# A hybrid decoder layer on one core: S5's four input tiles side by side, ahead of S5's tables

## The chip, the core and the metric

The kernel runs on one core of a Trainium2 chip. A core has a matrix engine (TensorE, here PE, with its weight loader PEld), a vector engine (VectorE, DVE), a scalar engine (ScalarE, ACT), a general engine (GpSimd, POOL) and a queue engine that issues most transfers (SyncE, SP). Each engine works through its own list of instructions; semaphores hold an instruction until what it reads is there. The metric is the time of one execution on the device in microseconds. The kernel before takes 1615.97 us, the median of three runs (1611.21 to 1623.19).

## The reference

One layer of a decoder trunk over a sequence of 1024 tokens of width 1024, all in float32. A normalised input is projected once; the columns of that projection feed an RWKV-7 branch, an S5 branch and two gates. The branches are merged, projected, normalised and added to the residual; a gated MLP with a short convolution follows. For the change only the first part matters:

```python
h = rms_norm(x, norm_mix_pre)
p = h @ w_in              # columns: RWKV's inputs | u (512 columns for S5) | two gates

def s5_branch(u, a_re, a_im, b_re, b_im, c_re, c_im, d, log_step, w_glu, b_glu):
    lam = lax.complex(a_re, a_im)
    dt = jnp.exp(log_step)[:, None]
    a_bar = jnp.exp(lam * dt)
    b_bar = ((a_bar - 1.0) / lam)[..., None] * lax.complex(b_re, b_im)
    ...
    _, states = lax.associative_scan(s5_combine, (a_elems, bu), axis=1)
    y = jnp.real(jnp.einsum('gcp,blgp->blgc', c, states)) + d * ug
```

`u` is 512 wide, that is four tiles of 128 channels. S5's coefficients (`a_bar`, its powers, `b_bar`, `c` times powers) depend on the parameters alone, not on x; the kernel calls what it derives from them "tables".

## The kernel before, in words

Activations lie transposed: 128 channels on the partitions, tokens along the row, in two halves of 512 tokens, `th` 0 and 1. A product of float32 accuracy is made from three matmuls of rounded operands: each operand is split into a high part (cast on ACT) and the low rest (a subtraction on DVE or POOL), and high x high, low x high and high x low are added in one PSUM bank (`mm3_steps`, the matmuls of L172, L173 and L174). So h of one half is eight tiles `hh` and eight `hl`, one pair for each of the eight k tiles of 128 channels, and a 128-column weight tile is `wh` and `wl`, each in two pieces of 512 (four k tiles apiece). The staging tile `wf` into which a piece is loaded has two buffers, `wh` and `wl` four each. An output tile of one half takes 8 x 3 = 24 matmuls of 128x512 into one of four banks called `gm`.

PE's order is written by a planner in the kernel; the other engines' order comes from a scheduler with priorities (HPN above HPW above HP2 above HP). The planner (`drive`, `background`, `drain`) runs **lanes** (generators that yield what a step costs on PE and how long to wait, the constants T_...) and puts **fill** between their steps: the list `self.fill` of generators, each step of it one k tile, three matmuls. `drain` runs fill until a condition holds.

The front half (`front_half`, from L1694) goes: norm of half 0, set-up and loading of S5's parameters, then a lane with the norm of half 1, during which fill begins. A norm squares x (ACT, sums of two on DVE), adds the squares over channels by matmuls with a column of ones (`sumsq`, L245), takes the root of the mean on DVE (`rstd`: L265, L136 to L141), spreads it over the partitions by matmuls (`spread`, L271), copies it out (`rbc`, L929) and scales x (L932), each tile then being split into `hh` (L226) and `hl` (L227). Fill begins with S5's input: `s5_in((0, 1))`, then `s5_in((2, 3))`, each of them two tiles of the first half of tokens, one behind the other, then the same two of the second; each tile's bank is copied out by ACT (`ev`, L1031), stored to `US`, and once both halves are stored, loaded again as `u8`. Behind it come `mix_in` (RWKV's input tiles), the gates' tiles, and the loads of the branch merge (`merge_loads`).

Behind the norm's lane stands `s5_setup`, many small DVE operations on 128x32 tiles, then S5's phase with two lanes: `tab_lane` makes tables (DVE from L508, transposes on PE at L544, L553, L598; trigonometry on DVE and ACT) and `s5_lane` runs the scan and the output products (L600 to L608 on DVE, L613 to L615 on PE). RWKV's phase follows (first matmul at L672, four "preps" and a chain; loads of its inputs go through ten buffers `ld`; last transposes of the output at L885), then the merge, the output projection, the next norm (L245 again), and the MLP.

Of the kernel before, what the change touches and what calls it, by code (L numbers as in the profile page):

```python
# [10 lines left out]
F32R = mybir.dt.float32r  # L11
# [7 lines left out]
D = 1024  # L19
T = 1024  # L20
NK = D // 128
# [50 lines left out]
class Kern:  # L72
# [68 lines left out]
            V.scalar_tensor_tensor(y, h, 1.5, y, ALU.add, ALU.mult)  # L141
        return y

    def load_w(self, *srcs):

        nc = self.nc
        wh, wl = [], []
        with self.tc.high_priority(HPW):
            for src in srcs:
                for o in range(0, src.shape[1], 512):  # L150
                    n = min(512, src.shape[1] - o)
                    h = self.wp.tile([128, 512], F32R, tag="wh", name=self.nm("wh"), bufs=NWH)
                    l = self.wp.tile([128, 512], F32R, tag="wl", name=self.nm("wl"), bufs=NWL)
                    f = self.wp.tile([128, 512], F32, tag="wf", name=self.nm("wf"), bufs=NWF)
                    nc.sync.dma_start(f[:, :n], src[:, o:o + n])
                    nc.scalar.copy(h[:, :n], f[:, :n])  # L156
                    nc.vector.tensor_tensor(l[:, :n], f[:, :n], h[:, :n].bitcast(F32), ALU.subtract)  # L157
                    wh.append(h)
                    wl.append(l)
        return wh, wl  # L160
# [753 lines left out]
    def norm(self, th, xs, pool):  # L914

        nc = self.nc
        ss = self.chk()[:, 0:512]
        yield 0, T_X
        for k in range(0, NK, 2):
            sq = [pool.tile([128, 512], F32, tag="sq", name=self.nm("sq"), bufs=4) for _ in range(2)]  # L920
            for i in range(2):
                nc.scalar.activation(sq[i], xs[k + i], AF.Square)
            nc.vector.tensor_tensor(sq[0], sq[0], sq[1], ALU.add)
            self.sumsq(ss, sq[0], k == 0)
            yield 0.9, 1.0
        bc = self.chk()[:, 0:512]
        self.spread(bc, self.rstd(ss, 1e-6, 1.0 / D))
        rbc = pool.tile([128, 512], F32, tag="rbc", name=self.nm("rbc"), bufs=1)
        nc.scalar.copy(rbc, bc)  # L929
        h = []  # L930
        for k in range(NK):
            nc.vector.scalar_tensor_tensor(xs[k], xs[k], self.vec("g_mix_pre", k), rbc, ALU.mult, ALU.mult)  # L932
            h.append(self.hsplit(xs[k], k, self.hp[th], eng=nc.gpsimd if k % 2 else nc.vector))
        self.h[th] = h
        yield 1.7, 5.0
# [84 lines left out]
        self.nc.sync.dma_start(self.u8[b], self.US[b].rearrange("i c g n -> (i c) g n"))  # L1020
        self.s5_in_done = b

    def s5_in(self, bs):

        w = [self.load_w(self.a["w_in"][14 + b]) for b in bs]
        for th in range(2):
            for b in bs:
                ps = self.gmp()
                yield from self.mm3_steps(ps, w[b % 2], 0, [h[0] for h in self.h[th]], [h[1] for h in self.h[th]])
                y = self.ev((128, 8, 64))  # L1030
                self.nc.scalar.copy(y.rearrange("p i n -> p n i"), ps.rearrange("p (n j) -> p n j", j=8)[:, :, ::-1])  # L1031
                self.nc.sync.dma_start(self.US[b].rearrange("i c g n -> (c g) i n")[:, :, th * 64:th * 64 + 64], y)
                if self.stored is not None:
                    self.load_u8(self.stored)
                    self.stored = None
                if th:
                    self.stored = b
# [656 lines left out]
    def front_half(self):  # L1694
# [7 lines left out]
        with tc.tile_pool(name="lxp", bufs=4) as self.lxp, tc.tile_pool(name="s5c", bufs=1) as self.s5c, \  # L1702
# [4 lines left out]
            with tc.tile_pool(name="xp", bufs=1) as xp:  # L1707
                with tc.high_priority(HPN):
                    xs = [self.load_x(0, xp)]
                    self.setup()  # L1710
                    self.s5w = {}
                    self.s5_load(0)
                    self.s5_load(1)
                    for _ in self.norm(0, xs[0], xp):
                        pass
                    xs.append(self.load_x(1, xp))
                self.fill = [self.s5_in((0, 1)), self.s5_in((2, 3)), self.mix_in()] + [self.gate_tiles(m) for m in range(14)] + [
                    self.merge_loads(), self.gate_tiles(14, 15)]
                self.outs, self.yr = 0, []
                self.drive([(HPN, self.norm(1, xs[1], xp))])  # L1720
                with tc.high_priority(HP):
                    self.s5_setup()
            with tc.tile_pool(name="s5p", bufs=1) as self.s5p:
# [63 lines left out]
                self.fill += [self.merge(mg), self.outproj(0, mg, self.mx0)]  # L1787


T_US, T_TAB0, T_TAB, T_TRIG, T_SCAN = 5.0, 38.0, 20.0, 12.0, 13.0  # L1790
T_LD, T_LT = 9.0, 3.0
NEVA = 4
T_KN, T_BK, T_GR, T_INV, T_LV, T_CH, T_LN = 5.0, 9.0, 2.5, 36.0, 1.0, 0.8, 11.0
T_X = 3.0
T_N0, T_RS, T_N1, T_N2, T_N4, T_N5, T_N3 = 2.5, 4.0, 2.2, 5.0, 1.6, 40.0, 2.0
NET = 5
MGAP = 1
# [2 lines left out]
NWH = 4  # L1800
NWL = 4
# [79 lines left out]
```

## Time and profile before

| what | value |
|---|---|
| median of three runs | 1615.97 us (1611.21 to 1623.19) |
| the profiled execution | 1613.51 us, of which its span 1611.7 us |
| mean granted clock of TensorE | 0.962 |
| PE busy | 1508.9 us (94%) |
| DVE busy | 1126.7 us (70%) |
| ACT busy | 696.8 us (43%) |
| POOL busy | 155.0 us (10%) |
| first matmul of S5's input | 25.92 us |
| S5's first table transposes (L544) | 106.2 us |
| RWKV's first product (L672) | 284.5 us |
| last transposes of RWKV's output (L885) | 781.4 us |

The profile is of one execution. A row of a timeline gives the start, the duration, the engine, the line, the operation, output and inputs, and in brackets the idle time before it with what ended it. A row of the stages gives from and to, the length, then for each engine the busy time with its count of instructions, then the clock granted to PE (1.00 is full speed), the busy share of the transfer engines and GB/s. A row of the waits gives what waited, for whom, and in total, how often and at longest. A matmul's duration overlaps the next one's, so the distance from start to start counts, not the duration.

### The profile page before, as it was taken

Reading aid. Unit: us, or ns where it says so; the run is one execution under the profiler, and the core shown is the slowest. Engines: PE = TensorE matmul, PEld = TensorE weight load, DVE = VectorE, ACT = ScalarE, POOL = GpSimd, SP = SyncE. Lnnn points to the kernel's source line nnn. Section 1 sums busy time; section 2 is a strip of 40 time slices with the busy share of each in tenths; the row PEclk is TensorE's granted clock in tenths of the full one; section 3 lists DMA queues with packets and bytes.
Section 4 is the critical chain, followed back from the end, with each engine's and each line's share of the span. In section 5 each row is a group of like instructions: output and inputs, shape, how many; then the busy total and the mean of one; then the engine's idle time right before and its main releaser. Section 6 shows DMA issues by size and latency. Waiting matters only on the chain. (4 is left out here: it accounts for less than half of the span.)

```text
span 1611.7 us, 26125 instructions
## 1 busy us (share of the span) xinstructions
PE 1508.9 (94%) x10028; PEld 1207.6 (75%) x10028; DVE 1126.7 (70%) x2039; ACT 696.8 (43%) x1109; POOL 155.0 (10%) x226
## 2 busy tenths in 40 slices
PE   5899899898999999889998999999999999999995
PEld 4688787686776776667866888788888887788784
DVE  5798774565365555865668579977777776788677
ACT  4345552224233344554443445554444444443451
POOL 2100001314123142010000000000000000000000
PEclk9799999999999999989988999999999999999997
DMA  5244334243352353552574453322222224963622
GB/s 178 63 140 142 98 113 169 65 136 117 106 153 94 97 171 107 171 156 93 190 223 156 144 190 125 124 79 83 90 89 78 78 87 142 321 215 106 229 84 104
DMA packets 133420, 213.84 MB, mean 133 GB/s; under 512 B 38656, under 2 KB 44800, under 8 KB 133296
## 3 DMA queue, kind: packets, MB, share of 16 engines
q1 hardware_dynamic: 124208, 188.32, 35.5%
q0 software_dynamic: 7936, 21.77, 4.6%
q10 hardware_dynamic: 1152, 2.10, 0.3%
q8 instruction: 78, 1.28, 0.3%
q14 instruction: 46, 0.38, 0.1%
HBM read 156.56 MB, written 53.48 MB: 130 GB/s over the span
## 5 line engine op out<-in xcount | busy, mean ns | idle before, releaser
L172 PE MATMUL gm<-hh,wh 128*128 128x512 f32 x688 | 299.6, 436 | 6.5 <-ACT hh L226 3.3
L173 PE MATMUL gm<-hl,wh 128*128 128x512 f32 x688 | 279.1, 406 | 5.4 <-DVE hl L227 4.5
L174 PE MATMUL gm<-hh,wl 128*128 128x512 f32 x688 | 276.6, 402 | 0.0
L156 ACT CAST wh<-wf 128x512 fp32r<-128x512 f32 x179 | 110.7, 620 | 196.7 <-PE gm L173 108.5
L157 DVE TENSOR_TENSOR wl<-wf,wh 128x512 fp32r<-128x512 f32 x179 | 124.8, 698 | 100.7 <-ACT wh L156 97.5
L172 PEld LDWEIGHTS gm<-hh,wh 128*128 128x128 f32 x688 | 134.0, 195 | 45.2 <-ACT hh L226 5.6
L173 PEld LDWEIGHTS gm<-hl,wh 128*128 128x128 f32 x688 | 134.2, 195 | 32.4 <-DVE hl L227 7.3
L174 PEld LDWEIGHTS gm<-hh,wl 128*128 128x128 f32 x688 | 134.1, 195 | 30.0
L1504 PE MATMUL d<-xl,wh 128*128 128x512 f32 x308 | 121.1, 393 | 3.3 <-DVE xl L227 3.3
L1503 PE MATMUL d<-xh,wh 128*128 128x512 f32 x308 | 120.8, 392 | 2.1 <-ACT xh L226 2.1
L1505 PE MATMUL d<-xh,wl 128*128 128x512 f32 x308 | 120.5, 391 | 0.0
L1329 PE MATMUL rp<-t,h 128*128 128x512 f32 x216 | 84.4, 391 | 1.9 <-ACT p L1343 1.9
L1331 PE MATMUL rp<-t,l 128*128 128x512 f32 x216 | 84.2, 390 | 0.5 <-DVE l L227 0.5
L1330 PE MATMUL rp<-t,h 128*128 128x512 f32 x216 | 84.1, 389 | 0.0
L1504 PEld LDWEIGHTS d<-xl,wh 128*128 128x128 f32 x308 | 58.1, 189 | 16.8 <-DVE xl L227 4.9
L1503 PEld LDWEIGHTS d<-xh,wh 128*128 128x128 f32 x308 | 58.2, 189 | 14.7 <-ACT xh L226 2.5
L1505 PEld LDWEIGHTS d<-xh,wl 128*128 128x128 f32 x308 | 58.2, 189 | 12.2
L226 ACT CAST h<-r 128x1024 fp32r<-128x1024 f32 x34 | 35.8, 1054 | 61.4 <-PE rp L1330 29.6
L227 DVE TENSOR_TENSOR l<-r,h 128x1024 fp32r<-128x1024 f32 x34 | 41.6, 1225 | 29.5 <-ACT h L226 28.0
L1350 DVE SCALAR_TENSOR_TENSOR y<-zv,vecs,y 128x1023 f32<-128x1023 f32 (+1 forms) x36 | 46.1, 1280 | 8.6 <-ACT y L1348 8.6
L1329 PEld LDWEIGHTS rp<-t,h 128*128 128x128 f32 x216 | 40.5, 188 | 11.4 <-ACT p L1343 2.7
L1331 PEld LDWEIGHTS rp<-t,l 128*128 128x128 f32 x216 | 40.5, 188 | 9.3 <-DVE l L227 1.0
(437 smaller groups left out, 3364.1 us busy)
## 6 DMA issues: line engine op xcount, KB each, us to landing
r<-in_w_up_dram SPq DMA_DIRECT2D x36, 512.0 KB, 3.2
wf<-in_w_in_dram SPq DMA_DIRECT2D x68, 256.0 KB, 2.9
st<-in_w_down_dram SPq DMA_DIRECT2D x55, 256.0 KB, 4.3
st<-ACT SPq DMA_DIRECT2D x44, 256.0 KB, 4.4
wf<-in_w_up_dram SPq DMA_DIRECT2D x36, 256.0 KB, 2.8
ACT<-y POOLq DMA_DIRECT2D x18, 512.0 KB, 2.9
GT<-ev SPq DMA_DIRECT2D x32, 256.0 KB, 2.3
wf<-in_w_br_dram SPq DMA_DIRECT2D x32, 256.0 KB, 3.1
```

The lines of the kernel that those rows point to most:

```text
L156: nc.scalar.copy(h[:, :n], f[:, :n])
L157: nc.vector.tensor_tensor(l[:, :n], f[:, :n], h[:, :n].bitcast(F32), ALU.subtract)
L172: mm(ps, a, xh[k], start=k == 0, stop=False)
L173: mm(ps, a, xl[k], start=False, stop=False)
L174: mm(ps, b, xh[k], start=False, stop=k == n - 1)
L1329: mm(ps, wh[:, c], xh, start=first and k == 0, stop=False, skip_group_check=True)
L1330: mm(ps, wh[:, c], xl, start=False, stop=False, skip_group_check=True)
L1331: mm(ps, wl[:, c], xh, start=False, stop=k == 3, skip_group_check=True)
L1350: V.scalar_tensor_tensor(y[:, lag:], z[:, 0:1024 - lag], self.vec(nme, i), y[:, lag:], ALU.mult, ALU.add)
L1503: mm(ps, wh[:, c], xh[:, x], start=start, stop=False, skip_group_check=True)
L1504: mm(ps, wh[:, c], xl[:, x], start=False, stop=False, skip_group_check=True)
L1505: mm(ps, wl[:, c], xh[:, x], start=False, stop=stop, skip_group_check=True)
```

## The change

`s5_in` handles all four tiles in one generator. It loads four weight tiles at the start (two of them into buffers of other pools: the high parts into the pool of x, the low parts into `lx` tiles), takes four banks for a half of the tokens, and goes over k outermost: at each k tile it steps through the four banks. When a half is done, the four banks are copied out and stored one behind the other. The norm's lane yields once between the root and its spread, with T_RS (4.0). After the norm's lane, fill is drained until the last tile of S5's input is finished, and only then comes `s5_setup`. Two constants change: the first wait of `norm`, T_X, and the first wait of the tables, T_TAB0.

```diff
-    def load_w(self, *srcs):
+    def load_w(self, *srcs, pool=None):
+        wp = pool or self.wp
...
-                    h = self.wp.tile([128, 512], F32R, tag="wh", name=self.nm("wh"), bufs=NWH)
-                    l = self.wp.tile([128, 512], F32R, tag="wl", name=self.nm("wl"), bufs=NWL)
+                    h = wp.tile([128, 512], F32R, tag="wh", name=self.nm("wh"), bufs=4 if pool else NWH)
+                    l = self.lx() if pool else wp.tile([128, 512], F32R, tag="wl", name=self.nm("wl"), bufs=NWL)
...
         bc = self.chk()[:, 0:512]
-        self.spread(bc, self.rstd(ss, 1e-6, 1.0 / D))
+        y = self.rstd(ss, 1e-6, 1.0 / D)
+        yield 0, T_RS
+        self.spread(bc, y)
...
-    def s5_in(self, bs):
-
-        w = [self.load_w(self.a["w_in"][14 + b]) for b in bs]
+    def s5_in(self, pool):
+
+        w = [self.load_w(self.a["w_in"][14 + b], pool=pool if b > 1 else None) for b in range(4)]
         for th in range(2):
-            for b in bs:
-                ps = self.gmp()
-                yield from self.mm3_steps(ps, w[b % 2], 0, [h[0] for h in self.h[th]], [h[1] for h in self.h[th]])
+            h = self.h[th]
+            ps = [self.gmp() for b in range(4)]
+            steps = [self.mm3_steps(ps[b], w[b], 0, [x[0] for x in h], [x[1] for x in h]) for b in range(4)]
+            for k in range(NK):
+                for b in range(4):
+                    yield next(steps[b])
+            for b in range(4):
+                next(steps[b], None)
                 y = self.ev((128, 8, 64))
-                self.nc.scalar.copy(y.rearrange("p i n -> p n i"), ps.rearrange("p (n j) -> p n j", j=8)[:, :, ::-1])
+                self.nc.scalar.copy(y.rearrange("p i n -> p n i"), ps[b].rearrange("p (n j) -> p n j", j=8)[:, :, ::-1])
...
-                self.fill = [self.s5_in((0, 1)), self.s5_in((2, 3)), self.mix_in()] + [self.gate_tiles(m) for m in range(14)] + [
+                self.fill = [self.s5_in(xp), self.mix_in()] + [self.gate_tiles(m) for m in range(14)] + [
                     self.merge_loads(), self.gate_tiles(14, 15)]
                 self.outs, self.yr = 0, []
                 self.drive([(HPN, self.norm(1, xs[1], xp))])
+                self.drain(lambda: self.stored == 3)
                 with tc.high_priority(HP):
                     self.s5_setup()
...
-T_US, T_TAB0, T_TAB, T_TRIG, T_SCAN = 5.0, 38.0, 20.0, 12.0, 13.0
+T_US, T_TAB0, T_TAB, T_TRIG, T_SCAN = 5.0, 20.0, 20.0, 12.0, 13.0
...
-T_X = 3.0
+T_X = 8.0
```

In the rows below a name's number tells one tile from another; in the kernel after the change the line numbers are higher by one up to L929, by three to about L1023 and by eight behind.

PE, the first matmuls of S5's input, before. `hh_301` and `hl_302` are the first k tile of h, `hh_306` and `hl_307` the second, `gm_381` the bank of the first output tile.

```order
L172 MATMUL gm_381<-hh_301,wh_357 128x512
L173 MATMUL gm_381<-hl_302,wh_357 128x512
L174 MATMUL gm_381<-hh_301,wl_358 128x512
L172 MATMUL gm_381<-hh_306,wh_357 128x512
L173 MATMUL gm_381<-hl_307,wh_357 128x512
L174 MATMUL gm_381<-hh_306,wl_358 128x512
```

PE at the same place, of the change (`gm_405` to `gm_408` are the four banks).

```order
L173 MATMUL gm_405<-hh_301,wh_357 128x512
L174 MATMUL gm_405<-hl_302,wh_357 128x512
L175 MATMUL gm_405<-hh_301,wl_358 128x512
L173 MATMUL gm_406<-hh_301,wh_369 128x512
L174 MATMUL gm_406<-hl_302,wh_369 128x512
L175 MATMUL gm_406<-hh_301,wl_370 128x512
L173 MATMUL gm_407<-hh_301,wh_381 128x512
L174 MATMUL gm_407<-hl_302,wh_381 128x512
L175 MATMUL gm_407<-hh_301,lx_382 128x512
L173 MATMUL gm_408<-hh_301,wh_393 128x512
L174 MATMUL gm_408<-hl_302,wh_393 128x512
L175 MATMUL gm_408<-hh_301,lx_394 128x512
```

A k tile of h is now read by twelve matmuls into four banks before the next one is wanted; before it was read by three.

ACT, from the copy of the spread root (`rbc`) of the second norm on, before: `hh_484` and those after it are the high parts of h's second half, `ev_424` and `ev_532` the copies of the first two banks.

```order
L1031 COPY ev_424<-gm_381 128x64x8
L929 COPY rbc_481<-chk_461 128x512
L388 ACT_TABLE_LOAD
L388 ACTIVATE sm_668<-sm_666 128x32
L389 ACTIVATE sm_670<-sm_666 128x32
L395 ACTIVATE sm_674<-sm_675 128x32
L390 ACTIVATE sm_669<-sm_670,hpi 128x32
L226 COPY hh_484<-x_340 128x512
L1031 COPY ev_532<-gm_427 128x64x8
L226 COPY hh_489<-x_342 128x512
L226 COPY hh_494<-x_344 128x512
```

ACT at the same place, of the change: `ev_603`, `606`, `609` and `612` are the copies of the four banks of the first half.

```order
L390 ACTIVATE sm_934<-sm_930 128x32
L391 ACTIVATE sm_933<-sm_934,hpi 128x32
L932 COPY rbc_543<-chk_505 128x512
L227 COPY hh_546<-x_340 128x512
L1039 COPY ev_603<-gm_405 128x64x8
L227 COPY hh_551<-x_342 128x512
L227 COPY hh_556<-x_344 128x512
L1039 COPY ev_606<-gm_406 128x64x8
L227 COPY hh_561<-x_346 128x512
L1039 COPY ev_609<-gm_407 128x64x8
L1039 COPY ev_612<-gm_408 128x64x8
L227 COPY hh_566<-x_348 128x512
```

The set-up's activations now stand ahead of `rbc`, and the four copies stand among the casts of h's second half.

DVE, where S5's tables begin, before: `sml` are the first products of the tables, `wl_914` a low part of a weight of RWKV's input.

```order
L508 TENSOR_TENSOR sml_824<-s_b_225,s5q_754 128x128
L509 TENSOR_TENSOR sml_825<-s_b_227,s5q_757 128x128
L557 TENSOR_TENSOR dg_1120<-csts,s5d 16x128
L510 TENSOR_TENSOR sml_821<-sml_824,sml_825 128x128
L157 TENSOR_TENSOR wl_914<-wf_915,wh_913 128x512
L508 TENSOR_TENSOR sml_829<-s_b_225,s5w_760 128x128
L509 TENSOR_TENSOR sml_830<-s_b_227,s5w_763 128x128
```

DVE at the same place, of the change (`wl_732` to `wl_1121` are the low parts of the first two weight tiles of RWKV's input).

```order
L475 TENSOR_SCALAR s5q_1005<-s5ai 64x288
L158 TENSOR_TENSOR wl_732<-wf_733,wh_731 128x512
L158 TENSOR_TENSOR wl_738<-wf_739,wh_737 128x512
L158 TENSOR_TENSOR wl_1115<-wf_1116,wh_1114 128x512
L158 TENSOR_TENSOR wl_1121<-wf_1122,wh_1120 128x512
L509 TENSOR_TENSOR sml_1020<-s_b_225,s5q_950 128x128
L510 TENSOR_TENSOR sml_1021<-s_b_227,s5q_953 128x128
L558 TENSOR_TENSOR dg_1217<-csts,s5d 16x128
```

Four weight pieces now stand in a row ahead of the tables' first product; before they stood among the products.

## The prediction

> **What bounds the kernel now.** I read the page's busy list first, then the stages, then the waits of the one stage that the change reorders.
>
> ```profile
> span 1611.7 us, 26125 instructions
> PE 1508.9 (94%) x10028; PEld 1207.6 (75%) x10028; DVE 1126.7 (70%) x2039; ACT 696.8 (43%) x1109; POOL 155.0 (10%) x226
> ```
>
> PE is the bound: 103 us of its span are idle or between instructions. The change adds and removes no matmul, so it can only win idle time or time at a lower clock. The stages (bounds chosen at the first matmul of h, the second norm's square sums, its scaling, the first unhindered matmul, S5's first table, RWKV's first product, its last transposes, the next norm):
>
> ```profile
> core 0: us, PE busy (x) PEld busy (x) DVE busy (x) ACT busy (x) POOL busy (x), PEclk, DMA share, GB/s
> 26.00:38.40 12.40, 10.69 (x29) 6.37 (x30) 12.40 (x15) 8.46 (x15) 5.62 (x4) 0.88 0.11 34
> 38.40:53.20 14.80, 14.35 (x52) 12.01 (x51) 8.29 (x74) 1.07 (x1) 0.48 (x1) 0.53 0.07 19
> 53.20:69.40 16.20, 11.30 (x34) 7.69 (x33) 14.58 (x35) 8.46 (x16) 5.56 (x4) 0.79 0.11 33
> 69.40:106.20 36.80, 36.80 (x164) 30.39 (x162) 35.34 (x90) 14.01 (x20) 0.89 (x2) 1.00 0.55 164
> 106.20:284.50 178.30, 168.07 (x926) 144.11 (x924) 124.08 (x188) 81.01 (x111) 13.54 (x22) 0.97 0.40 126
> 781.40:823.00 41.60, 38.25 (x157) 28.96 (x156) 22.84 (x33) 22.34 (x39) 0.00 (x0) 0.93 0.80 251
> ```
>
> The 43.4 us from 26.0 to 69.4 are the poor ones: PE busy 10.69, 14.35 and 11.30 us, clocks of 0.88, 0.53 and 0.79. Only 69 of S5's 192 input matmuls are done by 69.4. From there PE never stops and the clock is 1.00: 54 triplets' first matmuls in 36.80 us (next row), that is 162 matmuls at **0.2272 us**. That is the price of one "fill" matmul, the work the planner puts between the steps of a lane.
>
> ```profile
> 69.40:106.20 36.80, 21.04 (x54) 9.95 (x53) 1.00 0.55 164
> PE gm L173 <- DVE hl L227: 4.5, 5, 2.7
> PE gm L172 <- ACT hh L226: 3.3, 2, 2.1
> PE gm L173 <- POOL hl L227: 0.9, 1, 0.9
> PE chk L271 <- DVE sm L328: 0.5, 1, 0.5
> 45.65 0.63 PE L174 MATMUL gm<-hh,wl 128*128 128x512 f32 x1
> 46.08 0.63 PE L172 MATMUL gm<-hh,wh 128*128 128x512 f32 x1
> ```
>
> The waits (26 to 106 us) name h's halves as the releaser: 9.2 us with POOL's and the root's. The last two rows are 0.43 us apart: at the low clock a fill costs **0.427 us**.
>
> **The change, part by part.** *Where the fills go.* By the order, 231 fills stand ahead of S5's first transposes (L544) before and 285 after; ahead of the last output product of S5 (L613) 684 and 738; ahead of RWKV's first product (L672) 738 and 810; ahead of the last transposes L885 2049 and 2121; ahead of the next norm's square sums (L245) 2196 in both. So S5 and RWKV meet the same fills between their own steps, save 18 more just ahead of L672, and the last stretch has 72 fewer. The gain is therefore 72 x 0.2272 = 16.4 us, less what L885 comes later. I follow the delay to there.
>
> *First tile half (th0).*
>
> ```profile
> 25.92 0.79 PE L172 MATMUL gm<-hh,wh 128*128 128x512 f32 x1 [2.11 <-ACT hh L226]
> 27.20 0.80 PE L173 MATMUL gm<-hl,wh 128*128 128x512 f32 x1 [0.48 <-DVE hl L227]
> 34.22 0.95 PE L245 MATMUL chk<-ones,sq 128*128 128x1 f32 x8
> 38.82 1.70 PE L245 MATMUL chk<-ones,sq 128*128 128x1 f32 x8
> 49.09 0.16 DVE L265 TENSOR_SCALAR rv<-chk 128x4 f32<-128x4 f32 x1 [6.24 <-PE chk L245]
> 52.28 1.19 PE L271 MATMUL chk<-csts,rsy 128*128 128x128 f32 x8 [0.45 <-DVE sm L328]
> 54.12 2.08 DVE L932 SCALAR_TENSOR_TENSOR x<-x,vecs,rbc 128x512 f32<-128x512 f32 x3
> L157 DVE TENSOR_TENSOR wl<-wf,wh 128x512 fp32r<-128x512 f32 x179 | 124.8, 698 | 100.7 <-ACT wh L156 97.5
> ```
>
> Four more weight tiles are split ahead of h's scaling; two of their four lows stand among DVE's x rows, 0.7 us each, so I let the second matmul start at 27.9 instead of 27.2 (bounds 27.2 and 30.0, all four in series). Then each k brings 12 matmuls (2.7 us warm) where before it brought 3, and h's lows before came 1.6 us apart or less on average (the second at 27.2, the eighth's wait over at 37.80): after the first k nothing waits for h. Eleven fills at 0.427 lead to 32.6, the rest of the 96 at 0.2272 to 51.7; four square-sum groups at 0.95 and the spread at 1.19 make 56.7, with small change **57.1**. The root: its new wait of T_RS puts 24 fills (5.5 us) between the last square sums and the spread; on DVE it took from 49.09 to about 52.1 before, 3.0 us. So the root is covered, 0.5 us of wait goes, and what queues behind the spread on PE (6 fills, then the next tile's) waits for nothing new.
>
> *Bank handover.* DVE works through S5's small set-up ahead of the scaling of x (row 166 there, row 126 before). Spread at about 53, plus the copy of rbc, plus those rows, puts that scaling at 55.0, against 54.12: no earlier h for th1. And the four banks of th1 are those of th0, so each waits for its copy out:
>
> ```profile
> 56.06 0.60 ACT L226 CAST hh<-x 128x512 fp32r<-128x512 f32 x1
> L1031 ACT COPY ev<-gm x8: 1061/1092/1107, 42.0 to 99.2; 128x512 f32<-128x512 f32 x8
> ```
>
> ACT's order there is hh, copy, hh, hh, copy, hh, copy, copy. With 0.60 a cast (the first done at 56.3) and 1.09 a copy, they end at 57.4, 59.7, 61.4 and 62.5; the first k of th1 ends at **63.2** instead of 59.8, a new loss of 3.4 us. Behind it 84 x 0.2272 gives the 192nd fill at **82.3**; before it was 69.4 + 123 x 0.2272 = 97.3. L544 stands 93 fills on: **103.4**, against 106.2 (54 fills fewer).
>
> *S5's tables.* On DVE four weight lows now stand ahead of the tables.
>
> ```profile
> L156 ACT CAST wh<-wf 128x512 fp32r<-128x512 f32 x179 | 110.7, 620 | 196.7 <-PE gm L173 108.5
> wf<-in_w_in_dram SPq DMA_DIRECT2D x68, 256.0 KB, 2.9
> 76.83 0.29 DVE L508 TENSOR_TENSOR sml<-s_b,s5q 128x128 f32<-128x128 f32 x1
> 90.83 1.35 DVE L533 TENSOR_TENSOR ca<-ca,ct 128x1152 f32<-128x1152 f32 x1
> 131.61 1.23 DVE L600 TENSOR_TENSOR t<-chk,t 128x1024 f32<-128x1024 f32 x1 [4.04 <-ACT t L578]
> 140.45 1.22 DVE L608 TENSOR_TENSOR t<-t,t 128x1024 f32<-128x1024 f32 x1
> 145.82 0.39 PE L614 MATMUL chk<-t,ca 128*128 128x128 f32 x2
> ```
>
> The second low needs a wh whose buffer th1's last k reads until about 80; cast 0.62, low 0.70, then a load of 2.9 into the freed wf, cast and low again: 85.4. Tables that began at 76.83 begin there, 8.6 us late. The first ca took 15.4 us: 100.8, needed at 104: it holds. The rest catches up, since DVE had 4.04 us idle at 131.61 and six weight lows (4 us) that are done by then, so L608 ends near 143.9 (141.7 before), while PE, 2.8 earlier, asks at 143.0: **1 us** lost, of a margin that was 4.1.
>
> *To the end.* Delay at L885: -2.8 + 1 + 18 x 0.2272 (4.1) = +2.3. The 18 fills may hide a wait behind L672 (the largest below is 5.6); I count none. Ahead of L245 the stretch loses 16.4 of its 41.60 us, PE being busy 38.25 there; what it covers, the merge's split, keeps over 60 fills. **Gain 16.4 - 2.3 = 14.1.** The trace's execution took 1613.5 in all (span 1611.7), 2.5 below the median, so 1599.4 there and **1602** for the median of 1615.97. SP: two of the four new weight loads ahead of th1 stand inside s5_load, and two more of mix_in between the first three x of th1; each waits for one of wf's two slots, freed by a low on DVE, the last of them beside h's first scaling (about 26), so the rest of x goes out some 4 us later than before, to land by about 32. Their squares stand among ACT's hh casts, but after a k is wanted every 2.7 us from 32.6 on, where before one was wanted every 1.3, and the first square sum only at 38 (T_X): covered. If a late x did hold a cast, it would cost at most its load, 2.9. S5's own coefficients are wanted at 85. U's four stores in a row, then its loads, have 20 us until S5 asks. POOL keeps its h lows. These cost nothing; without that cover a late x would cost its 2.9.
>
> **The rivals.** *A: the low clock stays.* From 38.4 to 53.2 PE was busy 14.35 of 14.80 us and the clock was still 0.53, while square sums alternated with 6 fills. After does the same over 18 fills and four groups: held at the low clock, 18 x 0.200 + 4 x 0.75 = 6.6 us, and the later h hides none. Gain 7.5: 1608. The handover's waits (3.4 us in four pieces) can do the same for one span more. Against it: no square sum comes before fill 36. The Trainium skill ("TensorE: Matmul & The Clock Gate", Part 1, "What's actually happening") has a busy window of some 3.4 us release the clock, by which nothing of A would be paid; the rows of 38.4 to 53.2 disagree. The same page ("A second HAM failure mode: psum-queue depth-cycling") tells of a kernel that goes round its banks each iteration and loses the clock in small gaps, which speaks for A; no run here shows it yet.
>
> *B: the tables come later still.* The DVE row at 49.09 stood 6.24 us while small rows behind it were ready: a late weight holds all behind it. If the second weight load lands 5 us later than I put it (traffic of U), ca is late and L608 is 6 late: gain 8, 1608. The skill's same page ("Architectural detail") calls DVE's queue strict FIFO, and that row agrees.
>
> *C: better.* No handover loss (3.4), tables in time (1), one wait behind L672 hidden:
>
> ```profile
> PE rp L689 <- ACT gr L687: 9.4, 2, 5.6
> ```
>
> With none of the last the gain is 18.5, with half of 5.6 it is 21.3; I take 20: 1596.
>
> *D: slower.* The merge's loads of RWKV's output take slots of the ring "ld" ahead of the fourth prep's loads (behind them before), and a slot frees only when the branch is split into h's buffers, which gate 15's 48 fills still read. A split's two halves:
>
> ```profile
> L226 ACT CAST h<-r 128x1024 fp32r<-128x1024 f32 x34 | 35.8, 1054 | 61.4 <-PE rp L1330 29.6
> L227 DVE TENSOR_TENSOR l<-r,h 128x1024 fp32r<-128x1024 f32 x34 | 41.6, 1225 | 29.5 <-ACT h L226 28.0
> ```
>
> Worst, the fourth prep waits for those 10.9 us and four splits of 1.05 + 1.23 (9.1), 20 us in all, none covered: 1616 - 14 + 20 = 1622. It decides from 14 us on. Against it: by the order gate 15 begins 15 fills ahead of that prep, so 0 to 4 us is nearer. *E: the fills don't move:* the order shows them moved; 1616.
>
> **How the numbers follow.** Forecast (gain 11 to 17) 0.47, A 0.16, B 0.10, C 0.16, D 0.08, E 0.03. The range runs from C's 1596, less 2 for both at once, to 1618, between E and D's end: **1594 to 1618**. One per cent, 16.2 us, is about what a measurement of this kernel tells from none. Faster by more: C and a quarter of the forecast, 0.28; slower by more needs D with more behind it or a cause unseen, 0.07; within, 0.65.
>
> **What would show it.** Right: PE at clock 1.00 from 33 to 57; four waits on ACT's copies between 57 and 63; the 193rd fill (mix_in's first) near 82; L544 near 103; DVE idle before the tables until 85, behind ACT's wh; L672 about 2 us later than before and L885 too; L245 of the next norm near 809. Wrong: a clock of 0.5 after 38 (A); a wait of L553 or L614 for DVE over 3 us (B); waits of the fourth prep on SP's loads (D).

## The result, and the profile after

The changed kernel takes **1602.47 us** in the median of nine runs (1598.27 to 1607.13), beside 1614.95 for the kernel before, measured with it (nine runs): a ratio of 0.9921, with a 95% interval of 0.9904 to 0.9938, or 10.0 to 15.5 us. In two further measurements (e_after2, e_after3) the same kernel gave 0.9921 (0.9891 to 0.9951) and 0.9899 (0.9882 to 0.9916). The forecast was 1602, by a gain of 14.1 from 1615.97; the median moved by 12.5, the profiled span by 12.2.

The profile after, its first rows:

```profile
span 1599.5 us, 26116 instructions
PE 1501.5 (94%) x10028; PEld 1203.0 (75%) x10028; DVE 1130.4 (71%) x2039; ACT 694.0 (43%) x1107; POOL 154.9 (10%) x226
```

PE was busy 7.4 us less for the same matmuls: some of them ran at a higher clock. The stages of the changed kernel, with bounds at the first fill, the end of the first half, the end of the second half's first k tile, S5's first table transposes (now L545), RWKV's first product (L673), its last transposes (L886) and the next norm's square sums (L246):

```profile
core 0: us, PE busy (x) PEld busy (x) DVE busy (x) ACT busy (x) POOL busy (x), PEclk, DMA share, GB/s
26.53:55.74 29.21, 28.79 (x136) 23.74 (x136) 28.55 (x137) 13.56 (x26) 6.68 (x4) 1.00 0.22 66
55.74:61.19 5.45, 3.88 (x14) 2.13 (x14) 5.42 (x7) 5.27 (x9) 2.95 (x2) 1.00 0.50 128
61.19:101.40 40.21, 40.21 (x179) 33.23 (x178) 30.21 (x66) 16.82 (x25) 3.94 (x4) 1.00 0.47 142
101.40:283.30 181.90, 173.04 (x942) 147.54 (x941) 132.12 (x199) 76.91 (x106) 12.38 (x22) 0.97 0.40 128
283.30:781.10 497.80, 465.69 (x5288) 347.46 (x5287) 299.65 (x764) 198.40 (x426) 112.64 (x157) 0.96 0.41 122
781.10:806.00 24.90, 21.68 (x84) 15.70 (x83) 14.93 (x21) 13.81 (x24) 0.00 (x0) 0.87 0.79 240
```

Where the kernel before had clocks of 0.53 and 0.79 between 38.4 and 69.4, the changed one has 1.00 up to 101.4 us. The column says so too early, though: the trace holds no clock record before 31.4 us (31.9 in the kernel before), and the column counts that time as full. Until then the fills start 0.43 us apart in both kernels, the pitch of the half clock; from there on they start 0.23 us apart. The last stretch, 41.6 us before, is 24.9.

Five rows of PE's timeline and two of DVE's (start, duration, engine, line, operation, and in brackets the idle time before and what ended it):

```profile
27.75 0.79 PE L174 MATMUL gm<-hl,wh 128*128 128x512 f32 x1 [0.42 <-DVE hl L228]
31.33 0.44 PE L173 MATMUL gm<-hh,wh 128*128 128x512 f32 x1
...
50.73 1.05 PE L272 MATMUL chk<-csts,rsy 128*128 128x128 f32 x8
...
53.72 2.07 DVE L935 SCALAR_TENSOR_TENSOR x<-x,vecs,rbc 128x512 f32<-128x512 f32 x3
...
56.16 0.49 PE L173 MATMUL gm<-hh,wh 128*128 128x512 f32 x1 [0.27 <-ACT ev L1039]
...
58.05 0.50 PE L173 MATMUL gm<-hh,wh 128*128 128x512 f32 x1 [0.88 <-ACT ev L1039]
...
80.90 0.28 DVE L509 TENSOR_TENSOR sml<-s_b,s5q 128x128 f32<-128x128 f32 x1
```

The distance from fill to fill halves at 31.3; the spread of the root waits for nothing; the second half's first k tile waits for bank copies; the tables begin at 80.9. PE's waits from 24 to 106 us, and from 100 to 290:

```profile
PE gm L173 <- ACT hh L227: 2.1, 1, 2.1
PE gm L173 <- ACT ev L1039: 1.6, 3, 0.9
PE gm L174 <- DVE hl L228: 0.4, 1, 0.4
...
PE chk L615 <- DVE t L609: 4.4, 2, 2.4
PE chk L545 <- DVE t L601: 1.8, 1, 1.8
PE gm L173 <- DVE last L948: 1.7, 1, 1.7
PE chk L554 <- DVE t L602: 0.7, 1, 0.7
```

The 9.2 us of waits ahead of the tables have become 4.1, of which 2.1 stand ahead of the very first fill as before. In S5's phase there are 8.8 us, as against 10.2 before: other waits, not more of them.

How far the changed kernel's trace is ahead of that of before, at five places:

| place | before | after | measured lead | forecast |
|---|---|---|---|---|
| S5's first table transposes (54 more fills done) | 106.2 | 101.4 | 4.8 | 2.8 |
| RWKV's first product (72 more fills done) | 284.5 | 283.3 | 1.2 | -2.3 |
| RWKV's last transposes (72 more) | 781.4 | 781.1 | 0.3 | -2.3 |
| next norm's square sums (same fills) | 823.0 | 806.0 | 17.0 | 14.1 |
| end of the span | 1611.7 | 1599.5 | 12.2 | 14.1 |

So the gain does appear where the prediction put it, in the stretch that has 72 fills less to do, and it was earned ahead of 101 us. It is 2.9 larger there than forecast, and 4.8 of it are gone by the end.

### The profile page after: what moved, and what is told of

It is laid out like the page before. It is cut to its first block, busy times and chain, and to the rows that moved or that the text cites. A ratio compares the mean times of both kernels' runs of the same rounds, so it can differ in the third digit from the quotient of the medians.

```text
span 1599.5 us, 26116 instructions
## 1 busy us (share of the span) xinstructions
PE 1501.5 (94%) x10028; PEld 1203.0 (75%) x10028; DVE 1130.4 (71%) x2039; ACT 694.0 (43%) x1107; POOL 154.9 (10%) x226
## 4 chain that ended last, share of the span: by engine, by line
PE 57%; DVE 8%; DMA 3%; issue 1%; ACT 1%; POOL 0%; SPq 0%; DVEq 0%; ACTq 0%
PE gm L173 4%; PE rp L1337 4%; PE rp L1339 4%; PE rp L1338 4%; PE d L1512 4%; PE d L1511 4%; PE d L1513 4%; PE gm L174 3%; PE gm L175 3%; PE ch L173 2%; PE mm L1338 2%; PE mm L1337 2%; PE mm L1339 2%; PE ch L174 2%; PE ch L175 2%; PE mm L173 2%
## 5 line engine op out<-in xcount | busy, mean ns | idle before, releaser
L174 PE MATMUL gm<-hl,wh 128*128 128x512 f32 x688 | 275.1, 400 | 0.4 <-DVE hl L228 0.4
L175 PE MATMUL gm<-hh,wl 128*128 128x512 f32 x656 | 261.4, 398 | 0.0
L158 DVE TENSOR_TENSOR wl<-wf,wh 128x512 fp32r<-128x512 f32 x175 | 121.9, 697 | 103.4 <-ACT wh L157 83.1
L175 PEld LDWEIGHTS gm<-hh,wl 128*128 128x128 f32 x656 | 126.2, 192 | 28.6
L1511 PEld LDWEIGHTS d<-xh,wh 128*128 128x128 f32 x308 | 58.5, 190 | 16.2 <-ACT xh L227 2.5
L1513 PEld LDWEIGHTS d<-xh,wl 128*128 128x128 f32 x308 | 58.7, 191 | 12.2
L228 DVE TENSOR_TENSOR l<-r,h 128x1024 fp32r<-128x1024 f32 x34 | 41.6, 1225 | 29.4 <-ACT h L227 27.8
```

What stands on the lines that cost most here:

```text
L174: mm(ps, a, xl[k], start=False, stop=False)
L175: mm(ps, b, xh[k], start=False, stop=k == n - 1)
L1511: mm(ps, wh[:, c], xh[:, x], start=start, stop=False, skip_group_check=True)
L1513: mm(ps, wl[:, c], xh[:, x], start=False, stop=stop, skip_group_check=True)
```

## The experiments

The prediction's theory: PE's idle time and low clock between 26 and 69 us are won back, because each k tile of h now gives PE twelve matmuls. The first rival to it is that the **planner's** part pays: the wait behind the root, the drain, and 54 to 72 fills moved ahead. A second question concerns S5's tables and what holds them. Each ratio below is to the kernel before, measured beside the run.

**Only the four banks** (e_four). The kernel before with `s5_in` and `load_w` of the change:

```diff
-                self.fill = [self.s5_in((0, 1)), self.s5_in((2, 3)), self.mix_in()] + ...
+                self.fill = [self.s5_in(xp), self.mix_in()] + ...
```

> The kernel before with only S5's input done over four banks at once (four weight tiles loaded at the start, k outermost); no wait behind the root, no drain ahead of S5's set-up, T_X and T_TAB0 as before. PE's other work keeps its places among the fills (231 fills ahead of the first table transposes). Theory (the gain is PE's idle time and low clock between 26 and 69 us, and twelve matmuls for each k tile of h win it back): the 192nd fill near 83 us instead of 97, the first table transposes asked for near 92 instead of 106, and since DVE's tables cannot be so early, a wait there of 4 to 8 us; 8 to 12 us faster than before in all. Rival (the gain comes from the planner's part of the change, the wait behind the root and the places of the fills): at most 3 us faster.

Measured: 1616.15 us beside 1617.21 (0.9996; 0.9969 to 1.0022). No gain at all. Its window from 35 to 53 us, its waits from 90 to 290, DVE's first table product, and the first and last start of the table transposes and of RWKV's first products:

```profile
35.00:53.00 18.00, 16.04 (x86) 13.19 (x85) 17.42 (x66) 6.41 (x11) 6.65 (x4) 1.00 0.00 1
...
PE chk L554 <- DVE ca L534: 5.9, 1, 5.9
PE chk L615 <- DVE t L609: 5.1, 3, 2.2
PE gm L173 <- DVE ev L945: 3.2, 1, 3.2
PE gm L173 <- ACT ev L980: 2.5, 1, 2.5
...
85.69 0.28 DVE L509 TENSOR_TENSOR sml<-s_b,s5q 128x128 f32<-128x128 f32 x1
...
L545 PE MATMUL chk<-csts,t x32: 272/273/422, 94.3 to 219.8; 128*128 128x128 f32 x32
L673 PE MATMUL rp<-csts,gr x32: 166/251/272, 283.6 to 387.1; 128*128 128x2 f32 x32
```

The front did what the theory said: full clock, and the transposes at 94.3 instead of 106.2, with the same 231 fills ahead of them. But the 11.9 us are down to 0.9 at RWKV's first product. Its four largest waits in S5's phase come to 16.7, where all of those before were 10.2: the tables are asked for 12 us earlier, and DVE begins them 8.9 us later than before (85.69 instead of 76.83). The theory foresaw the wait and thought it 4 to 8 us; it took everything. By its time alone the rival's condition (at most 3 us faster) is met; what decides against it is that the planner's part alone brings nothing either (e_bdrain, below).

**Two banks instead of four** (e_pairs). The kernel before, each pair over two banks:

```diff
-                ps = self.gmp()
-                yield from self.mm3_steps(ps, w[b % 2], 0, ...)
+            ps = {b: self.gmp() for b in bs}
+            steps = {b: self.mm3_steps(ps[b], w[b % 2], 0, ...) for b in bs}
+            for k in range(NK):
+                for b in bs:
+                    yield next(steps[b])
```

> The kernel before with each pair of S5's input tiles done over two banks at once (six matmuls for each k tile of h instead of three), nothing else. Theory: the first half's h no longer holds PE, but only 48 fills stand ahead of the second half's h, so the wait for the second norm stays; its eight k tiles come every 1.6 us with 1.4 us of work each, so 69.4 us has about 96 fills done instead of 69, 27 x 0.2272 = 6 us; 3 to 7 us faster than before. Rival (planner's part): within 2 us of before.

Measured: 1605.82 beside 1617.21 (0.9918; 0.9892 to 0.9944), as much as the whole change. Its windows, and the same two rows as above:

```profile
26.00:35.00 9.00, 8.52 (x38) 6.91 (x38) 9.00 (x12) 6.17 (x13) 3.97 (x3) 1.00 0.12 34
35.00:53.00 18.00, 15.23 (x76) 11.91 (x75) 16.99 (x62) 7.97 (x13) 5.49 (x5) 1.00 0.11 29
...
L544 PE MATMUL chk<-csts,t x32: 270/273/273, 94.5 to 210.5; 128*128 128x128 f32 x32
L672 PE MATMUL rp<-csts,gr x32: 165/251/272, 272.6 to 376.0; 128*128 128x2 f32 x32
```

Six matmuls for each k tile are enough for the clock: 76 matmul records from 35 to 53 us at 1.00, where the kernel before had 56 at 0.53. So the second norm comes earlier too (its spread at 42.6 instead of 52.3), which the expectation had left out; hence 11.7 us at the transposes instead of the 3 to 7 expected. And here they are kept: 11.9 at RWKV's first product. What differs from the four banks is where DVE's tables begin: at 69.8 us (76.8 before, 85.7 in e_four). The pair kernel gives the pool of x back when h is done; with four banks that pool holds two of the four weights until the last input matmul.

**Only the planner's part** (e_bdrain). The kernel before with the drain and T_TAB0 of the change:

```diff
+                self.drain(lambda: self.stored == 3)
-T_US, T_TAB0, T_TAB, T_TRIG, T_SCAN = 5.0, 38.0, 20.0, 12.0, 13.0
+T_US, T_TAB0, T_TAB, T_TRIG, T_SCAN = 5.0, 20.0, 20.0, 12.0, 13.0
```

> The planner's part of the change alone: the kernel before, tile by tile as it was, with the drain ahead of S5's set-up and T_TAB0 at 20, so that 285 fills stand ahead of the first table transposes and 2121 ahead of RWKV's last ones, as in the changed kernel; no four banks, no wait behind the root, T_X as before. Theory (the gain is the idle time and the low clock of 26 to 69 us, which this leaves alone): first table transposes at 118 us, at most 3 us faster than before from waits in S5's phase. Rival (more cover ahead of S5's tables is what pays): 5 us or more faster than before.

Measured: 1619.47 beside 1617.29 (1.0006; 0.9993 to 1.0019): nothing. Window and rows:

```profile
35.00:53.00 18.00, 17.14 (x57) 13.46 (x58) 11.48 (x84) 2.65 (x5) 1.60 (x1) 0.54 0.06 16
...
L544 PE MATMUL chk<-csts,t x32: 270/272/301, 117.7 to 235.3; 128*128 128x128 f32 x32
L672 PE MATMUL rp<-csts,gr x32: 165/251/354, 295.9 to 395.1; 128*128 128x2 f32 x32
```

The front is as slow as before, and PE does 285 fills ahead of the transposes instead of 231: 117.7. Moving fills earns nothing by itself. RWKV's first product stands 5.0 us better than 284.5 and 72 fills (16.4) would give, yet nothing of it is seen in the medians.

**Pairs and the planner's part** (e_pdrain), the two diffs above together.

> The pairs over two banks (six matmuls for each k tile) with the same planner's part. The pairs alone were 0.9918 of the time before. Theory (the front's gain of some 11 us is kept whatever the fills' places are, as long as the tables are in time): 0.988 to 0.993 of the time before, within 4 us of the changed kernel. Rival (four banks are needed beside the moved fills): 5 us or more slower than the changed kernel.

Measured: 1605.26 beside 1617.29 (0.9918; 0.9899 to 0.9936), the same as the pairs alone. With e_four and the changed kernel that makes a table of the two parts:

| S5's input | fills as before | fills moved |
|---|---|---|
| one bank at a time | 1 | 1.0006 |
| two banks | 0.9918 | 0.9918 |
| four banks | 0.9996 | 0.9921, 0.9921, 0.9899 |

Two banks pay without the move; four pay with it only. The move alone is no source of the gain: it is what the four banks need. That they need it because their tables come late is argued from e_four's waits; four banks with the tables early and the fills where they were, which would show it, were not run. The changed kernel's cell also has the wait behind the root, worth nothing by e_noyield, and T_X at 8, which was not tried alone.

**Without the drain** (e_nodrain), the changed kernel less one line.

```diff
-                self.drain(lambda: self.stored == 3)
```

> The changed kernel without the drain ahead of S5's set-up (the first table transposes stand at fill 192 instead of 285). Theory: PE asks for the tables at about 80 us, DVE has them near 95 to 100; a wait of 12 to 18 us there, most of it not won back: 8 to 16 us slower than the changed kernel. Rival (the drain only changes the order, since the fills skipped are done later behind other waits): within 4 us of the changed kernel.

Measured: 1629.41 beside 1617.21 (1.0067; 1.0043 to 1.0091). Against 0.9921 of the changed kernel that is some 24 us; the direction is the theory's, the size above it. The waits from 60 to 290:

```profile
PE chk L615 <- DVE t L609: 9.1, 2, 5.1
PE chk L545 <- issue: 8.4, 1, 8.4
PE chk L554 <- DVE ca L534: 3.8, 1, 3.8
```

The transposes stand at 88.3, 192 fills on. DVE begins the tables at 80.4, when those fills are done, and PE stands 8.4 us (the view names no releaser) and 3.8 us until the tables are there, then 9.1 more for the scan. It reaches RWKV's first product at 283.2, about when the changed kernel does (283.3), but with 714 fills done instead of 810: 96 x 0.2272 = 21.8 us behind, so nearly all of the loss is made ahead of there.

**Without the wait behind the root** (e_noyield).

```diff
         y = self.rstd(ss, 1e-6, 1.0 / D)
-        yield 0, T_RS
         self.spread(bc, y)
```

> The changed kernel without the wait between the root of the second norm and its spread (the spread stands at fill 60 instead of 78). Theory: PE stands 1.6 to 2.5 us for the root, but h of the second half then comes about 2 us earlier and the bank handover's 3.7 us of waits shrink by as much; within 2 us of the changed kernel. Rival (the wait behind the root is worth its 3 us or more): 3 to 5 us slower than the changed kernel.

Measured: 1605.20 beside 1617.21 (0.9910; 0.9884 to 0.9937), where the changed kernel has 0.9899 to 0.9921. PE then waits 1.8 us for the root, the spread comes at 49.1 instead of 50.7 and the first cast of the second half at 51.7 instead of 54.5, but the waits for bank copies grow from 1.6 to 2.5 us. The wait behind the root is worth nothing that can be measured, as the theory had it.

**What holds the tables** (e_u8). The high weights of the last two tiles in the buffers of u8, which are empty until S5's input has been stored, instead of in the pool of x:

```diff
-                    h = wp.tile([128, 512], F32R, tag="wh", ..., bufs=4 if pool else NWH)
+                    h = wp.tile([128, 512], F32R, tag="wh", ..., bufs=NWH) if into is None else \
+                        into[:, o // 128:o // 128 + 4].rearrange("p a b -> p (a b)").bitcast(F32R)
```

> The changed kernel with the high weight parts of the last two of S5's input tiles in the buffers of u8 (free until S5's input is stored) instead of in the pool of x. Theory (S5's tables lie in the memory that the pool of x gives back, and wait for the last matmul that reads a weight there, 79 us): with the pool free at about 65 us the tables begin by 70 us, the waits for tables between 101 and 190 us go, and 4 to 7 us are won on the changed kernel (ratio to before near 0.988). Rival (the tables are late because weight lows of RWKV's input stand ahead of them in DVE's queue, or the waits behind 101 us are of another origin): the tables begin no earlier than 78 us, and the time is within 2 us of the changed kernel.

Measured: 1602.77 beside the changed kernel's 1602.59 (0.9911, 0.9880 to 0.9943, and 0.9921). The first table product and RWKV's first product; then, of the changed kernel, the last two of the four weight lows that stand ahead of its tables (DVE's timeline):

```profile
67.41 0.29 DVE L510 TENSOR_TENSOR sml<-s_b,s5q 128x128 f32<-128x128 f32 x1
...
L674 PE MATMUL rp<-csts,gr x32: 165/251/373, 278.0 to 380.3; 128*128 128x2 f32 x32
```

```profile
78.85 0.69 DVE L158 TENSOR_TENSOR wl<-wf,wh 128x512 fp32r<-128x512 f32 x1 [8.21 <-PE gm L174]
80.29 0.69 DVE L158 TENSOR_TENSOR wl<-wf,wh 128x512 fp32r<-128x512 f32 x1 [0.74 <-ACT wh L157]
```

The tables begin at 67.4 instead of 80.9, ahead of all four weight lows that stood in front of them. The edit moves only the two weights' high parts, so the loan of the pool's memory is what puts the tables late. The trace of the changed kernel doesn't show the memory as what DVE stands for: it stands 8.21 and 0.74 us for the third and fourth low, and the tables follow at once. The two come to the same time: the last matmul that reads a borrowed tile starts at 79.81, the lows are through at 80.9. So without the lows the tables could have begun about 0.7 us earlier at most (an estimate: 79.81 and the matmul's 0.39 make 80.2). The wait for the scan at L616 falls to 2.4 us and RWKV begins at 278.0, 4.0 ahead of the changed kernel's profile beside it (282.0). But the time is the same. Measured once more:

> The kernel with the weights in u8 again, in five rounds. It reaches RWKV's first product 4 us ahead of the changed kernel. Theory (what is won there reaches the end; what its first profile lost behind was low-clock windows that fall where they fall): 3 to 5 us faster than the changed kernel over the medians. Rival (RWKV's phase takes it back in its own waits): no faster than the changed kernel.

1601.88 beside the changed kernel's 1601.37 (0.9895 and 0.9899, each to within about 0.0017). The theory's 3 to 5 us did not come; the lead at RWKV's first product was only 1.4 us in this profile. By its condition the rival holds (no faster), but its mechanism is not shown: RWKV's phase ran at a clock of 0.94 in both profiles of this kernel and at 0.96, 0.94 and 0.95 in the three of the changed one. Where a lead of 1 to 4 us goes stays open.

**Bank by bank at the end** (e_u8s). The last four k tiles of each half are done one bank after the other:

```diff
-            for k in range(NK):
+            for k in range(NK - 4):
                 for b in range(4):
                     yield next(steps[b])
             for b in range(4):
+                for k in range(4):
+                    yield next(steps[b])
```

> As the one with the weights in u8, and the last four k tiles of each half done bank by bank, so that the four banks end 2.7 us apart and are copied out one by one. Theory: the waits for bank copies (1.6 us in three) go and PE waits only for the first cast of the second half (up to 2.1 us); 1 to 2 us faster than without it. Rival (the handover is bounded by the second half's h alone): no difference.

Measured: 1604.03 (0.9929; 0.9900 to 0.9957), no difference. From 50 to 66 us the waits for bank copies fall from 1.7 to 1.2 us and waits for h of 1.2 appear: the handover is bounded by h as much as by the copies. The rival had it bounded by h alone, which isn't shown: 1.2 us of copies are left.

**More fills ahead of the tables** (e_tab38). The changed kernel with T_TAB0 at 38.

> The changed kernel with T_TAB0 as before (38): the first table transposes stand at fill 363 instead of 285, everything up to them as in the changed kernel. Theory: asked for 17.7 us later, the tables are in time, and PE reaches RWKV's first product with the 5 to 7 us that the changed kernel loses between 101 and 190 us still won; but only 15 fills are left in the last stretch ahead of the next norm's square sums, too few for what the merge needs, which gives back 4 to 10 us: within 4 us of the changed kernel in all. Rival (the waits behind 101 us don't come from late tables): the same waits at L545 to L615 as in the changed kernel.

Measured: 1610.40 beside the changed kernel's 1602.59, 7.8 us slower by the medians. The ratios (0.9957, 0.9930 to 0.9984, and 0.9921, 0.9891 to 0.9951) lie some 5.8 us apart and their intervals just overlap, but nine of its ten runs are slower than the slowest of the changed kernel's six (1606.00). RWKV's first product, then the largest waits of RWKV's phase:

```profile
L673 PE MATMUL rp<-csts,gr x16: 165/251/251, 288.9 to 290.5; 128*128 128x2 f32 x16
...
PE rp L886 <- DVE yn L880: 13.6, 1, 13.6
PE gm L173 <- ACT hh L227: 11.7, 1, 11.7
...
596.82 0.72 ACT L669 ACTIVATE gr<-ld,vecs 128x512 f32<-128x512 f32 x1 [5.16 <-DMA ld<-RKV]
```

78 more fills stand ahead of the transposes, and 72 (16.4 us) ahead of RWKV's first product. It reaches that only 5.6 to 7.0 us later than the three profiles of the changed kernel, so the waits of S5's phase are indeed won (3.2 us of them are left). But the fills then reach the branch merge while the fourth prep is still at its loads: the merge's first fill waits 11.7 us, until 600, for the cast of RWKV's output into h's buffers, which stands on ACT behind the prep's instruction that waits 5.2 us for its load (last row, ACT's timeline); the last transposes wait 13.6. The expectation looked for the price behind RWKV's last transposes and put it at 4 to 10; it came ahead of them. This is where the prediction's rival D begins: not in the changed kernel, but 78 fills further.

**The changed kernel twice more** (e_after2, e_after3).

> The changed kernel once more, to be compared with the next three on the same chip, and for a second profile of it. Both theories: 0.990 to 0.994 of the time before; in its profile the first table transposes near 101 us; what the first profile lost behind 870 us against the kernel before (4.8 us) is not there again in the same places if it came from where the low-clock windows fell.

> The changed kernel again, in five rounds beside the next three. 0.990 to 0.994 of the time before. A third profile of it: PE reaches RWKV's first product within 2 us of the first two (283.3 and 282.0), and the rest of the span differs by the low-clock windows.

Measured: 1602.59 and 1601.37. The first table transposes come at 102.3 and 100.8 and RWKV's first product at 282.0 and 281.9. RWKV's last transposes, and the clock from 290 to 790 us, of the first and the second:

```profile
L886 PE MATMUL rp<-csts,yn x8: 272/272/273, 787.9 to 788.6; 128*128 128x128 f32 x8
290.00:790.00 500.00, 466.87 (x5264) 347.83 (x5265) 291.21 (x750) 196.98 (x424) 104.24 (x150) 0.94 0.42 121
```

```profile
L886 PE MATMUL rp<-csts,yn x8: 272/272/273, 783.9 to 784.6; 128*128 128x128 f32 x8
290.00:790.00 500.00, 465.75 (x5282) 347.51 (x5283) 293.40 (x754) 199.41 (x427) 105.07 (x151) 0.95 0.43 123
```

RWKV's phase takes 497.8, 505.9 and 502.0 us in three executions of one program, at clocks of 0.96, 0.94 and 0.95; the longest has 61 us at half clock between these places, the shortest 44. And from the next norm's square sums (813.7 and 809.5) to the end it loses 1.2 and 1.4 us against before where the first profile lost 4.8. So a single profile tells the front to about 2 us and everything behind RWKV only to about 8.

## Why the prediction was right, and where it was not

The time was right (1602 forecast, 1602.5 measured), and so was the ground of it: the gain comes from the idle time and the clock between 26 and 69 us. What the runs add is that two banks win it alone, and that the rest of the change is not needed for it. That forecast and median meet within half a microsecond is partly luck: the changed kernel was 17.0 us ahead at the next norm's square sums where 14.1 were forecast, then lost 4.8 that nobody forecast, and the median of the kernel before was 1614.95 this time and not 1615.97. And the prediction took one per cent, 16.2 us, for what a measurement tells from none; the interval here is 5.5 us wide. Step by step:

- **First half.** Second fill at 27.75 (27.9 forecast), low pitch until 31.3 (32.6), four square-sum groups and the spread without a wait, end at 55.7 (57.1). The rows held: 0.2272 a fill, and 0.9 a square-sum group where its duration, 0.95, had been put (0.81 from its start to the next fill's, and that fill takes 0.1 longer).
- **Rival A did not come.** The alternation of square sums and six fills that stood at 0.53 before runs at 1.00. The pairs show it with the square sums at the same fills as before (the first behind fill 15), so the alternation alone doesn't lower the clock; whether it keeps a clock that is low already from rising is not shown. The Trainium skill ("TensorE: Matmul & The Clock Gate", Part 1, "What's actually happening") would have given this forecast, and the changed kernel agrees with it: the full-clock pitch comes 4.8 us after the first fill (26.53 to 31.33). Its warning about cycling through banks ("A second HAM failure mode: psum-queue depth-cycling") does not show here: four banks in turn keep 1.00 (31.4 to 101.4 us).
- **The root's wait** was costed at 0.5 us won, and e_noyield finds no more.
- **Bank handover.** 2.7 us lost (5.45 less 12 x 0.2272), 3.4 forecast. The transposes come at 101.4 instead of the forecast 103.4, for the sum of these.
- **S5's tables: the start was near, the cause half seen.** The step put the tables behind four weight lows and the weights' buffers, at 85.4. DVE does stand for the third and fourth low, but the further load of 2.9 us that the step counted is not waited for, and the tables begin at 80.9. What the step missed is the loan of the pool of x, which e_u8 shows to be what makes the tables late at all. What it cost was small, as said: from the transposes to RWKV's first product the lead falls by 3.6, against 5.1 forecast (1 for the tables and 4.1 for the 18 fills). But the step missed how much hangs on it: without the 54 moved fills tables as late eat all of the front's gain (e_four). The prediction counted the moved fills as the place where the gain is seen and did not ask what the four banks would give without them.
- **Twelve matmuls for a k tile** were given as the reason that h no longer holds PE. Six do nearly as well (e_pairs; PE's waits for h from 24 to 106 us are 3.9 us there and 2.5 in the changed kernel, 2.1 of each ahead of the first fill), with none of the rest.
- **The last stretch.** 41.6 to 24.9 us, 16.7 shorter, where 72 x 0.2272 = 16.4 was forecast: right.
- **Behind it** nothing was forecast. The lead falls from 17.0 to 12.2 in the first profile, and by 1.2 and 1.4 in the others. In the medians the gain is 12.5, 12.6 and 15.9.
- **Rival B's** sign, a wait of L614 (now L615) for DVE over 3 us, came in the third profile (4.0; 2.4 in the first two), but not its cause: the tables began at 80.3 there.
- **Rival C** came in part: PE's waits at L689 behind RWKV's first product fell from 9.4 us to 3.4, 3.2 and 4.8. RWKV's phase is no shorter for it (496.9 us before, 497.8 to 505.9 after).
- **Rival D** was rightly held small: PE's largest waits in RWKV's phase are 11.4 (L794) and 6.3 us (L885) before, 12.8 and 7.9 in the first profile after. e_tab38 shows its price, when the fills run ahead of the branch: 11.7 and 13.6 us.

## What to carry to other kernels

When an engine waits tile by tile for a producer, give it more work for each arrival: two accumulators were enough here, and every one more costs buffers that somebody else wants. Ask of any weight or tile put into borrowed memory who gets that memory next; here the loan moved S5's tables by 13 us (e_u8), and the four banks that needed it gained nothing until the planner put more work ahead of the tables. And a lead is not a gain until the next consumer's inputs are early too: compare it at several places of the trace, at equal work.

## What was not expected of the hardware

The low clock of the kernel before is not explained by how busy PE was. From 35 to 53 us PE was busy 17.13 us of 18 at a clock of 0.53; the pairs, with the same square sums among the same fills, were busy 15.23 of 18 at 1.00:

```profile
35.00:53.00 18.00, 17.13 (x56) 13.30 (x56) 11.48 (x76) 2.94 (x4) 1.94 (x2) 0.53 0.06 16
```

Nor does the stretch ahead settle it: from 26 to 35 us PE was busy 7.71 us of 9 before and 8.52 in the pairs, but only 7.28 in the changed kernel without the wait behind the root, and that kernel kept 1.00 from 35 to 53 us. In the kernel before the clock fell at 35.3 us, behind a wait for h of 0.72 us and the first square-sum group; in the pairs waits of 1.64 and 0.91 us, at 42.6 and 46.7, left it at 1.00. The Trainium skill ("TensorE: Matmul & The Clock Gate", Part 1, "What's actually happening") has one busy window of about 3.4 us lift the clock; here PE stayed at half clock for 17 us while it was busy 95% of the time. That busy time counts the three square-sum groups, 1.70 us each with matmuls one column wide, as it counts the fills; whether the clock gate does was not tried. That e_bdrain does the same (17.14 of 18, 0.54) shows that it belongs to the order of the work and not to one execution. What lifts the clock or keeps it low in this case stays open.
